# Layer 0's projections as quads of quarter products with a spill to DRAM, and the heads as a second stage

## The chip, the cores and the metric

One Trainium2 chip, of which the kernel uses one core. Times are microseconds of the device for one execution. The engines of a core are named as in the profile: PE is TensorE (matmuls), PEld its weight loads, DVE is VectorE, ACT ScalarE, POOL GpSimd and SP SyncE, whose queue issues most transfers. A mask, a weight or a state lives in SBUF, results of matmuls in PSUM, and everything else in DRAM (HBM).

## The reference

A backbone of two layers over 512 latent tokens (x, 1024 features) and 256 context tokens (ctx). Layer 0 is a retention with four heads, of 256 features for q and k and 512 for v; latent tokens read context and latent tokens in both directions, so that its recurrent form is the same as one product with a mask of decays. Layer 1 is a chunked gMLP with gates. Only x leaves the kernel, so the context passes through layer 0's k and v alone.

```python
for i in range(DEPTH):
    ...
    shift_x, scale_x, gate_x = jnp.split(silu_c @ ada_w[i] + ada_b[i], 3, axis=-1)
    hx = rmsnorm(x, norm_g[i]) * (1 + scale_x[:, None]) + shift_x[:, None]
    hc = rmsnorm(ctx, norm_g[i]) * (1 + scale_c) + shift_c
    ...
    x = x + gate_x[:, None] * out_x
return rmsnorm(x, final_g)

def retention_mixer(hx, hc, w_in, decay_logit, w_out, need_ctx):
    ...
    qc, kc, vc, zc = retention_project(hc, w_in)
    qx, kx, vx, zx = retention_project(hx, w_in)
    qx, kx = axial_rope(qx, row, col), axial_rope(kx, row, col)
    ...
    ox, _, _ = retention_bidirectional(qx, kx, vx, log_g, s_f, s_b)
    out_x = retention_output(ox, zx, w_out)

def retention_output(o, z, w_out):
    o = o * lax.rsqrt(jnp.mean(o * o, axis=-1, keepdims=True) + NORM_EPS)
    ...
    return (o * jax.nn.silu(z)) @ w_out
```

## The kernel before

All data are float32. A factor of a product is split into a high part (a cast to fp32r, on ACT) and a low part (the rest, a subtraction on DVE; `split`, line 86), and `mm3` (line 80) makes each product of three matmuls: low by high, high by low, high by high. So a split of a tile of 128 × 1024 weights costs one operation of ACT and one of DVE.

Weights come in one stream (`Stream`, line 103): a tile is loaded into one of four raw buffers, split into one of four "hl" buffers, two tiles ahead of their use. Layer 0 goes head by head (the loop at line 643). For a head, `proj_v` (414) multiplies the weights of v with the features of x and ctx (`hx`, `hc`, split once), eight steps of 128 over the 1024 features, 512 columns at a time; `proj_z` (433) does the gate's z. `attend` (461) makes scores of 128 keys by 256 queries (twelve for a head, 6 matmuls of 256 columns each), multiplies each with the mask (`pf`), splits it (`phl`), and three scores later multiplies it with v (512 columns); `finish` normalises and gates (`gt`), and `flip` transposes into `og`. `proj_q` of the next head comes next, then `project_out` (535), 96 matmuls of 512 columns for a head (in the last head two halves of 256), whose results DVE adds to the residual `acc`, then `proj_k`. The masks of a head (`decay`, 451) are made by ACT and POOL one head ahead.

The first q and k are made apart, in `proj_qk_first` (339), while layer 0's modulation is still computed: for each of eight blocks of 128 features, PE makes the block's shift and scale (`ada0_mm`, 16 records of `ada_w`), transposes them, and multiplies the finished block with four weight tiles.

In the background (`background`, 590) 32 more tiles of adaLN weights (512 KB each) are loaded one by one and accumulated by DVE (`ada_piece`, 560): a multiplication of 128 × 1024 each, four pieces of eight tiles. They give layer 0's gate and layer 1's shift, scale and gate. `step` moves this on by one tile; it is called once for each weight tile of v and z, and once or twice between.

Layer 1's input projections already use a scheme of seven products in place of eight (`Quads`, 782, and the tables `USES` and `SINGLE`, 776 to 780): both factors are cut into quarters, sums and differences of quarters are formed (T1 to T4 of the weights, S1 to S4 of x), seven products of quarters are made, and their results are combined. The differences of weights, the combinations and the splits fall to DVE and ACT.

The order of the work on PE, ACT and DVE in layer 0 is set by the tile scheduler, which keeps the order of the text only where an engine is marked `kept`; a queue of DMA issues, and each engine, then works its rows in that order.

## Time and profile before

| what | value |
|---|---|
| median of three runs (lowest, highest) | 939.91 us (939.73, 944.60) |
| the profiled execution's own time | 943.52 us |
| its span, first to last instruction | 941.7 us |
| mean granted TensorE clock | 0.989 |
| PE, DVE, ACT, POOL busy | 922.0, 618.5, 385.4, 83.6 us |
| HBM traffic | 117.05 MB read, 8.39 MB written |
| matmuls of PE from 121 to 146 us (the first attention) | 25.00 of 25.00 us busy |

The profile is that of one execution. A row of a group reads: source line, engine, operation, output <- inputs, shapes, how many | busy time, mean ns of one | idle time of the engine just before them, and what ended most of it. Nearly every row has line 53, the helper that records each operation, so groups are told apart by the names of tiles. In a timeline a row gives start and length of a run of like instructions; records of matmuls overlap, so that the rate is read from start to start. In a window a row gives, for each engine, the busy time and the number of instructions, then the granted clock, the DMA share and GB/s.

### The profile page before, as it was taken

To read this page: it belongs to the slowest core of one execution; us is meant where nothing else is said; L and a number is where in the kernel's file an instruction comes from. 1 tells how busy PE (TensorE), PEld (TensorE's weight loads), DVE (VectorE), ACT (ScalarE), POOL (GpSimd) and SP (SyncE) were. 2 spreads that over 40 slices of the span, in tenths; PEclk is the share of its full clock that TensorE was granted. 3 is DMA by queue.
4 is the path that set the end of the run, shared out by engine and by line. 5 is a ranking of instruction groups with operands and counts; after the bars stand their busy time and mean duration, and the time that the engine had idled before them with its cause. 6 is when DMAs were issued, how large, how long until landed. Compare 5 with 4: busy or idle time off the path is not lost.

```text
span 941.7 us, 13689 instructions
## 1 busy us (share of the span) xinstructions
PE 922.0 (98%) x5474; PEld 797.2 (85%) x5474; DVE 618.5 (66%) x895; ACT 385.4 (41%) x606; POOL 83.6 (9%) x64
## 2 busy tenths in 40 slices
PE   8899999999999999999999999899999999999997
PEld 6578887888787887888887899899999899899885
DVE  4575746653348554248454467999999668788975
ACT  4344435222235212344112447755455355244244
POOL 1413102300003100005000000110100000000000
PEclk8899999999999999999999999999999999999999
DMA  9914813544204544205544202474543335136102
GB/s 355 362 63 122 283 74 112 182 133 155 90 1 143 175 141 144 68 1 179 179 134 155 69 23 95 165 256 138 187 136 124 112 99 183 33 113 222 47 23 90
DMA packets 49424, 126.33 MB, mean 134 GB/s; under 512 B 5456, under 2 KB 13776, under 8 KB 49232
## 3 DMA queue, kind: packets, MB, share of 16 engines
q1 hardware_dynamic: 47440, 119.16, 37.8%
q0 software_dynamic: 1920, 6.29, 1.7%
q8 instruction: 43, 0.70, 0.3%
q14 instruction: 21, 0.17, 0.1%
HBM read 117.05 MB, written 8.39 MB: 133 GB/s over the span
## 4 chain that ended last, share of the span: by engine, by line
PE 74%; DMA 10%; DVE 10%; issue 2%; ACT 2%; POOL 1%; SPq 0%; DVEq 0%; POOLq 0%; ACTq 0%
PE pst L53 74%; DMA raw<-in_adag_dram 8%; DVE hl L53 3%; DMA raw<-in_w_dram 1%; DVE rope_t L53 1%; DMA acc<-in_xT_dram 1%; POOL raw L53 1%; ACT hl L53 1%; DVE fz L53 1%; DMA raw<-in_dec_dram 0%; DVE q L53 0%; DVE ada_a L53 0%; ACT f L53 0%; POOL dec L53 0%; DVE ya L53 0%
## 5 line engine op out<-in xcount | busy, mean ns | idle before, releaser
L53 DVE TENSOR_TENSOR hl<-raw,hl 128x1024 fp32r<-128x1024 f32 (+1 forms) x115 | 144.9, 1264 | 66.8 <-ACT hl L53 66.1
L53 ACT CAST hl<-raw 128x1024 fp32r<-128x1024 f32 x115 | 120.1, 1049 | 166.1 <-PE pst L53 94.8
L53 PE MATMUL pst<-hl,hx 128*128 128x512 f32 x696 | 167.4, 395 | 0.9 <-DVE v L53 0.8
L53 PEld LDWEIGHTS pst<-hl,hx 128*128 128x128 f32 x696 | 130.0, 187 | 33.5 <-DVE v L53 2.1
L53 PE MATMUL pst<-hx,hl 128*128 128x512 f32 x384 | 105.1, 407 | 2.0 <-ACT hx L53 1.7
L53 PE MATMUL pst<-hs,hl 128*128 128x256 f32 x768 | 94.7, 282 | 0.0
L53 PEld LDWEIGHTS pst<-hs,hl 128*128 128x128 f32 x768 | 92.4, 188 | 0.3
L53 PE MATMUL pst<-og,hl 128*128 128x512 f32 (+1 forms) x480 | 91.9, 351 | 0.0
L53 PEld LDWEIGHTS pst<-og,hl 128*128 128x128 f32 x480 | 77.0, 188 | 13.8 <-DVE og L53 0.7
L53 DVE SCALAR_TENSOR_TENSOR ada_a<-raw,cpad,ada_a 128x1024 f32<-128x1024 f32 x28 | 37.0, 1320 | 76.9 <-DMA raw<-in_adag_dram 76.8
L53 PEld LDWEIGHTS pst<-hx,hl 128*128 128x128 f32 x384 | 69.0, 192 | 19.6 <-issue 4.4
L53 PE MATMUL pst<-hl,ya 128*128 128x512 f32 x288 | 71.8, 402 | 2.2 <-DVE ya L53 2.2
L53 PE MATMUL pst<-s,hl 128*128 128x256 f32 x576 | 70.5, 280 | 0.0
L53 PEld LDWEIGHTS pst<-s,hl 128*128 128x128 f32 x576 | 69.0, 188 | 0.1
L53 PEld LDWEIGHTS pst<-hl,ya 128*128 128x128 f32 x288 | 55.0, 192 | 15.5 <-DVE ya L53 2.6
L53 POOL TENSOR_TENSOR raw<-raw 128x1024 f32<-128x1024 f32 x12 | 31.8, 2647 | 327.2 <-DMA raw<-in_dec_dram 291.6
L53 PE MATMUL pst<-v,phl 128*128 128x512 f32 x192 | 49.2, 394 | 0.0
L53 DVE SCALAR_TENSOR_TENSOR pf<-pst,dec 128x256 f32<-128x256 f32 x48 | 19.9, 422 | 42.3 <-PE pst L53 42.3
L53 ACT CAST hl<-rx 128x1024 fp32r<-128x1024 f32 x27 | 28.3, 1049 | 29.9 <-DVE rx L53 16.8
L53 PE MATMUL pst<-hl,hs 128*128 128x256 f32 x336 | 40.1, 280 | 0.1
L53 PE MATMUL pst<-hl,hc 128*128 128x512 f32 x156 | 40.1, 395 | 0.0
L53 PEld LDWEIGHTS pst<-hl,hs 128*128 128x128 f32 x336 | 39.5, 188 | 0.3 <-DVE hl L53 0.3
(204 smaller groups left out, 1288.3 us busy)
## 6 DMA issues: line engine op xcount, KB each, us to landing
raw<-in_w_dram SPq DMA_DIRECT2D x64, 512.0 KB, 3.6
raw<-in_w_dram SPq DMA_DIRECT2D x72, 256.0 KB, 3.3
raw<-in_adag_dram SPq DMA_DIRECT2D x32, 512.0 KB, 4.5
raw<-in_dec_dram SPq DMA_DIRECT2D x24, 512.0 KB, 3.6
rx<-in_w_dram SPq DMA_DIRECT2D x36, 256.0 KB, 3.8
ada_w<-in_ada_dram SPq DMA_DIRECT2D x16, 512.0 KB, 8.0
vt<-snap POOLq DMA_DIRECT2D x16, 256.0 KB, 3.8
rkc<-in_w_dram SPq DMA_DIRECT2D x16, 256.0 KB, 3.9
```

The source lines that it names most:

```text
L53: made = op(*args, **kw)
```

## The change

Layer 0's projections become a stage of their own. A list of twelve quads (`QUADS`) goes through the scheme of seven products: one quad for q and k of a head (`features`), two for the halves of v and z of a head (`tokens`). Every product is 24 matmuls of 256 columns. Two of the seven (B11, B21) have a second product beside them with the context as the other factor (`beside`), for k and v of the context. Results are split once (`staged`, four buffers g0 to g3) and stored to DRAM by transfers that POOL issues; for q and k the rotation is done first (`kq_finish`).

The start is rewritten: x is loaded as four quarters, the sums of squares are 48 matmuls of one column (`norm`, three times 16) instead of six, 20 more filling matmuls stand between them, and the loop over the eight blocks of features feeds B11 and B21 of the first three quads, for x (`xs`) and the context (`cs`).

Then the heads follow as a second stage. `load_qk` and `load_v` fetch a head's operands from DRAM, v into the tiles oA11, oS1 and oS2, z into oA12, the same for each head. `attend` makes two scores at a time, 512 columns wide in PSUM (two banks, "tm"), with two such pairs of lag; `project_out` is always two halves of 256 columns, on six banks ("ps"). The adaLN pieces 1 to 3 (24 tiles) move into `attend` and `project_out`, through the two raw buffers w2 and w3; each output weight passes through the raw buffer w0. Masks are made by ACT and DVE; POOL keeps no tensor operation. Layer 1 stays as it was, but for the names of buffers and the common weight stream.

```diff
-            q = proj_q(rest)
-            step(1)
-            dt = st([P, TW], "dec")
-            parts = decay(h + 1, dt)
-            for _ in project_out(og, 1, parts):
-                pass
-            kk_ = proj_k()
...
+    QUADS = (("vz", 0, 0), ("vz", 0, 1), ("vz", 1, 0), ("vz", 1, 1), ("kq", 0), ("vz", 2, 0), ("kq", 1), ("vz", 2, 1),
+             ("kq", 2), ("vz", 3, 0), ("kq", 3), ("vz", 3, 1))
+    first3 = QUADS[:3]
...
+    def tokens(bank, a, w, fresh, ks=range(4)):
+        for kt in ks:
+            r = (w[:, 0, kt * HS:kt * HS + HS], w[:, 1, kt * HS:kt * HS + HS])
+            for t in range(2):
+                l = (a[:, 0, kt, t * P:t * P + P], a[:, 1, kt, t * P:t * P + P])
...
+        def beside(self, name, w):
+            if self.side is None:
+                return
+            if name == "B11":
+                self.c = pt()
+                self.product(self.c, self.side[:, :, 0:4, :], w, True)
+            else:
+                self.product(self.c, self.side[:, :, 4:8, :], w, False)
+                self.done("c", self.c)
...
+    def norm(pair, tags):
+        sqs = [st([P, 4, HS], tag, name="sq0") for tag in tags]
+        act.activation(sqs[0], pair[0], AF.Square)
...
+            for k in range(4):
+                for t in range(2):
+                    mm(p[:, t:t + 1], sqs[g][:, k, t * P:t * P + P], ones[:, 0:1], start=(g, k, t) == (0, 0, 0),
+                       stop=(g, k) == (1, 3), skip_group_check=True)
...
+    def staged(src):
+        t = st([P, 2, 512], f"g{turn[0] % 4}", F32R, name="stg")
+        turn[0] += 1
+        split((t[:, 0, :], t[:, 1, :]), src)
+        return f32(t)
...
+    def kq_finish(h, name, c):
+        if name == "c":
+            spill(kc_d[h], staged(c).rearrange("p a b -> p (a b)"))
+            return
...
+        two = lambda x: x.rearrange("p (m t) -> p m t", m=2)
+        a, b = t2("rope_a"), t2("rope_b")
+        for x, w in ((a, 0), (b, 1)):
+            dve.tensor_tensor(two(x), two(c), rope[:, w, sl].unsqueeze(1).to_broadcast([P, 2, HS]), ALU.mult)
+        dve.tensor_tensor(a[:, 0:HS], a[:, 0:HS], b[:, HS:], ALU.subtract)
+        dve.tensor_tensor(a[:, HS:], a[:, HS:], b[:, 0:HS], ALU.add)
+        spill(dst[h][th], staged(a).rearrange("p a b -> p (a b)"))
...
+    def vz_done(h, fh):
+        fs = slice(fh * HS, fh * HS + HS)
+        def done(name, c):
+            if name in ("11", "21", "c"):
+                dst = vc_d[h] if name == "c" else v_d[h][int(name[0]) - 1]
+                s = staged(c)
+                for x in range(2):
+                    spill(dst[:, x, :, fs], s[:, x, :].rearrange("p (t n) -> p t n", t=2))
+                return
+            act.activation(c, c, AF.Silu)
+            spill(z_d[h][int(name[0]) - 1][:, :, fs], c.rearrange("p (t n) -> p t n", t=2))
...
+    for kb in range(1, 8):
+        if kb == 4:
+            for pr in prods:
+                pr.snap("s1", pr.x)
+        xs(kb)
+        next(n1, None)
...
+    def ada_piece(i, tag, tags):
+        a = st([P, D], tag, name="ada_a")
+        rows = []
+        for k in range(KT + 1):
+            if k < KT:
+                rows.append(bg_raw(tags))
+                load(rows[k], adag_d[8 * i + k])
+            if k == 0:
+                yield None
...
+    def load_qk(h):
+        tags = ("s0", "s1", "s2", "s3", "rope") if h % 2 == 0 else ("w4", "w5", "w6", "g2", "g3")
+        t = [st([P, 2, 2, HS], tag, F32R, name="qk") for tag in tags]
+        for x, src in zip(t, (k_d[h][0], q_d[h][0], k_d[h][1], kc_d[h], q_d[h][1])):
+            load(f32(x).rearrange("p a b c -> p (a b c)"), src)
+        qk[h] = (t[1], t[4]), (t[0], t[2]), t[3]
...
+    def load_v(h):
+        v = [st([P, 2, 2, 512], tag, F32R, name="v") for tag in ("oA11", "oS1", "oS2")]
+        z = st([P, NT, 512], "oA12", name="z")
+        for x, src in zip(v, (*v_d[h], vc_d[h])):
+            load(f32(x), src)
+        for t in range(2):
+            load(z[:, 2 * t:2 * t + 2, :], z_d[h][t])
+        vv[h] = v, z
...
+    for n, q in enumerate(QUADS[3:]):
+        pr = project(q)
+        for i, name in enumerate(SINGLE):
+            pr.run(name, Q.get())
+            if later and i % 2:
...
+            p = pt(tag="tm")
+            for o in range(2):
+                src, jj = key(j + 1 - o)
+                for m in range(2):
+                    l = (src[:, 0, m, jj * P:jj * P + P], src[:, 1, m, jj * P:jj * P + P])
+                    mm3(p[:, o * HS:o * HS + HS], l, (q[hf][:, 0, m, :], q[hf][:, 1, m, :]), m == 0, m == 1)
...
+        LAG = 2
...
+            if i > 2:
+                Q.upto(Q.at + min(i - 1, 5))
+            if i >= LAG:
+                step()
+        return og, flip
...
+    def project_out(og, flip, parts, then=None, between=None, prepare=None):
+        ws = []
+        for hf in range(2):
+            sl = slice(hf * HS, hf * HS + HS)
             for c in range(4):
                 if hf == 0:
...
+                if then is None:
+                    step()
+                    if c == 3:
+                        step()
...
+    for h in range(HEADS - 1):
+        og, flip = attend(h)
+        load_qk(h + 1)
+        load_v(h + 1)
+        project_out(og, flip, decay(h + 1))
+    og, flip = attend(HEADS - 1)
```

By the order of instructions, matmuls of 512 columns go from 2307 to 674, those of 256 from 2689 to 5664, those of one column from 6 to 48 and of 128 from 211 to 237. DVE's operations of 128 × 1024 on two tensors go from 224 to 327, those of 128 × 512 from 213 to 295. POOL loses 36 tensor operations and goes from 24 to 108 DMA issues.

Three places show the new order. First PE in the projections. Before, in and after head 0's attention (v, phl: values; hx, hl: q of head 1; og, hl: the output projection):

```order
L53 MATMUL pst<-q,kc 128x256 x6
L53 MATMUL pst<-v,phl 128x512 x12
L53 MATMUL pst<-vc,phl 128x512 x12
L53 MATMUL pst<-ada_a,ones 32x512 x2
L53 MATMUL pst<-hx,hl 128x512 x24
L53 MATMUL pst<-ident,gt 128x128 x16
L53 MATMUL pst<-hx,hl 128x512 x24
L53 MATMUL pst<-ident,cole 128x64 x4
L53 MATMUL pst<-og,hl 128x512 x96
```

Now, one whole quad of v and z in the first stage (oA and oS are the quarters of x and their sums, hc the context, hl the weights):

```order
L53 MATMUL pst<-oA_190,hl 128x256 x24
L53 MATMUL pst<-hc,hl 128x256 x24
L53 MATMUL pst<-oS_687,hl 128x256 x24
L53 MATMUL pst<-oS_870,hl 128x256 x24
L53 MATMUL pst<-oA_574,hl 128x256 x24
L53 MATMUL pst<-hc,hl 128x256 x24
L53 MATMUL pst<-oS_688,hl 128x256 x24
L53 MATMUL pst<-oS_871,hl 128x256 x24
L53 MATMUL pst<-oA_872,hl 128x256 x24
```

What were runs of 24 to 96 matmuls of 512 columns are now nine products of 24 matmuls of 256, two of them for the context.

Second, DVE where the loop over the blocks of the start has ended. Before, it splits weights and the first kc, and rotates the first q and k:

```order
L53 TENSOR_TENSOR hl_z<-raw,hl_z 128x1024
L53 TENSOR_TENSOR hl_v<-raw,hl_v 128x1024
L53 TENSOR_TENSOR kc<-pst,kc 128x256 x2
L53 TENSOR_TENSOR rope_t<-pst,rope 128x512 x4
L53 TENSOR_TENSOR rope_t<-rope_t 128x512
L53 TENSOR_TENSOR q<-rope_t,q 128x512
L53 TENSOR_TENSOR rope_t<-rope_t 128x512
L53 TENSOR_TENSOR q<-rope_t,q 128x512
L53 TENSOR_TENSOR rope_t<-pst,rope 128x512 x4
L53 TENSOR_TENSOR rope_t<-rope_t 128x512
L53 TENSOR_TENSOR k<-rope_t,k 128x512
L53 TENSOR_TENSOR rope_t<-rope_t 128x512
```

Now (xq are the quarters of x, oS and oA the low parts of their sums, c and stg the first results, combined and split for the store, hl weights):

```order
L53 TENSOR_TENSOR xq<-xq 128x512
L53 TENSOR_TENSOR c_884<-pst,snap 128x512
L53 TENSOR_TENSOR xq<-xq 128x1024
L53 TENSOR_TENSOR oS_687<-xq,oS_687 128x512
L53 TENSOR_TENSOR stg<-c_884,stg 128x512
L53 TENSOR_TENSOR oS_870<-xq,oS_870 128x1024
L53 TENSOR_TENSOR hl<-raw,hl 128x1024
L53 TENSOR_TENSOR stg<-pst,stg 128x512
L53 TENSOR_TENSOR xq<-xq 128x1024
L53 TENSOR_TENSOR oA_872<-xq,oA_872 128x1024
L53 TENSOR_TENSOR c_901<-pst,snap 128x512
L53 TENSOR_TENSOR oS_871<-xq,oS_871 128x1024
```

and directly on, up to the split of the weights of T3 of the first quad:

```order
L53 TENSOR_TENSOR stg<-c_901,stg 128x512
L53 TENSOR_TENSOR stg<-pst,stg 128x512
L53 TENSOR_TENSOR c_913<-pst,snap 128x512
L53 TENSOR_TENSOR stg<-pst,stg 128x512
L53 TENSOR_TENSOR hl<-raw,hl 128x1024
```

The forming of the quarters' sums and the first results of three quads stand ahead of that weight split.

Third, the heads. Before, DVE in the output projection of head 0 (acc: residual; ada_a on raw: adaLN tile; hl: weights):

```order
L53 SCALAR_TENSOR_TENSOR acc<-pst,gate_118,acc 128x512 x2
L53 TENSOR_TENSOR hl<-raw,hl 128x1024
L53 SCALAR_TENSOR_TENSOR acc<-pst,gate_118,acc 128x512 x2
L53 TENSOR_TENSOR hl<-raw,hl 128x1024
L53 SCALAR_TENSOR_TENSOR acc<-pst,gate_118,acc 128x512 x2
L53 TENSOR_SCALAR ada_a<-raw,cpad 128x1024
L53 TENSOR_TENSOR hl<-raw,hl 128x1024
L53 SCALAR_TENSOR_TENSOR acc<-pst,gate_118,acc 128x512 x2
L53 SCALAR_TENSOR_TENSOR ada_a<-raw,cpad,ada_a 128x1024
L53 TENSOR_TENSOR hl<-raw,hl 128x1024
L53 SCALAR_TENSOR_TENSOR ada_a<-raw,cpad,ada_a 128x1024
L53 TENSOR_TENSOR rope_t<-pst,rope 128x512
```

Now, DVE in head 0's attention (pf: score by mask; pl: its low part; ada_a on bg: adaLN tile):

```order
L53 SCALAR_TENSOR_TENSOR pf<-pst,dt 128x512
L53 TENSOR_TENSOR hl<-raw,hl 128x1024
L53 TENSOR_TENSOR pl<-pf,ph 128x512
L53 SCALAR_TENSOR_TENSOR pf<-pst,dt 128x512
L53 SCALAR_TENSOR_TENSOR ada_a<-bg,cpad,ada_a 128x1024
L53 TENSOR_TENSOR pl<-pf,ph 128x512
L53 SCALAR_TENSOR_TENSOR pf<-pst,dt 128x512
L53 SCALAR_TENSOR_TENSOR ada_a<-bg,cpad,ada_a 128x1024
L53 TENSOR_TENSOR pl<-pf,ph 128x512
```

and DVE in the output projection of head 0:

```order
L53 SCALAR_TENSOR_TENSOR acc<-pst,gate_925,acc 128x256 x3
L53 TENSOR_TENSOR og<-pst,og 128x512 x2
L53 SCALAR_TENSOR_TENSOR acc<-pst,gate_925,acc 128x256 x2
L53 SCALAR_TENSOR_TENSOR ada_a<-bg,cpad,ada_a 128x1024
L53 TENSOR_TENSOR dt<-bg 128x512
L53 SCALAR_TENSOR_TENSOR ada_a<-bg,cpad,ada_a 128x1024
L53 TENSOR_SCALAR ada_a<-bg,cpad 128x1024
L53 SCALAR_TENSOR_TENSOR ada_a<-bg,cpad,ada_a 128x1024
L53 SCALAR_TENSOR_TENSOR acc<-pst,gate_925,acc 128x256 x2
L53 COPY sh_927<-pst 128x8
L53 TENSOR_TENSOR sh_927<-sh_927,sv 128x8
L53 TENSOR_TENSOR shs<-sh_927 128x4
```

and the loads on SP's queue for the change from head 0 to head 1 (v, z: head 1's; raw: output weights; bg: adaLN tile or mask):

```order
L108 DMA v<-v_172 128x2048
L108 DMA raw<-in_w_dram 128x1024
L108 DMA v<-v_173 128x2048
L108 DMA v<-vc_179 128x2048
L108 DMA z<-z_184 128x1024
L108 DMA z<-z_185 128x1024
L108 DMA bg<-in_adag_dram 128x1024
L108 DMA bg<-in_dec_dram 128x1024
L108 DMA bg<-in_adag_dram 128x1024 x2
```

The adaLN multiplies, which stood one between two weight splits, now stand up to four together between the residual's additions, and between a score and its low part; their loads stand behind those of the next head's v and z.

1163 lines of the change are left out of this document (555 added, 608 removed).

## The prediction

> **What bounds the kernel now.** I read the table of engines and the slices first, then the chain of waits, then the groups of instructions, and last the timeline and the windows of the stages that the change touches.
>
> ```profile
> PE 922.0 (98%) x5474; PEld 797.2 (85%) x5474; DVE 618.5 (66%) x895; ACT 385.4 (41%) x606; POOL 83.6 (9%) x64
> GB/s 355 362 63 122 283 74 112 182 133 155 90 1 143 175 141 144 68 1 179 179 134 155 69 23 95 165 256 138 187 136 124 112 99 183 33 113 222 47 23 90
> PE 74%; DMA 10%; DVE 10%; issue 2%; ACT 2%; POOL 1%; SPq 0%; DVEq 0%; POOLq 0%; ACTq 0%
> L53 PE MATMUL pst<-hl,hx 128*128 128x512 f32 x696 | 167.4, 395 | 0.9 <-DVE v L53 0.8
> L53 PE MATMUL pst<-hs,hl 128*128 128x256 f32 x768 | 94.7, 282 | 0.0
> ```
>
> TensorE (PE) is busy for 922.0 us of a span of 941.7 waits before almost no group, and carries 74% of the chain that ended last, so work taken from it comes off the time, unless another engine then falls behind. VectorE (DVE) stands at 66%; transfers reached 355 and 362 GB/s in two slices, against a mean of 134.
>
> Since records of matmuls overlap, the price of one comes from stretches without a gap:
>
> ```profile
> 506.53 22.65 PE L53 MATMUL pst<-hl,hx 128*128 128x512 f32 x96
> 529.02 3.03 PE L53 MATMUL pst<-q,k 128*128 128x256 f32 x24
> 555.21 8.68 PE L53 MATMUL pst<-og,hl 128*128 128x256 f32 x72
> 563.72 1.04 PE L53 MATMUL pst<-ident,acc 128*128 128x128 f32 x8
> ```
>
> From start to start, 96 of 512 columns take 22.49 us (0.234 each) and 72 of 256 take 8.51 (0.118 each): half the width costs half the time. A product of quarters, 24 matmuls of 256 columns, is 2.84 us.
>
> How far DVE can be loaded before PE waits is read from the windows:
>
> ```profile
> core 0: us, PE busy (x) PEld busy (x) DVE busy (x) ACT busy (x) POOL busy (x), PEclk, DMA share, GB/s
> 0.00:57.00 57.00, 49.55 (x307) 33.99 (x307) 29.53 (x70) 23.87 (x44) 14.17 (x15) 0.88 0.77 297
> 620.00:740.00 120.00, 119.87 (x998) 118.36 (x998) 114.06 (x162) 60.78 (x81) 7.05 (x13) 1.00 0.50 169
> 756.20:799.40 43.20, 43.20 (x369) 43.20 (x368) 35.87 (x45) 21.48 (x30) 0.00 (x0) 1.00 0.45 146
> ```
>
> Layer 1 already works in products of quarters, and PE stays full with DVE at 83% (756 to 799) and even at 95% (620 to 740).
>
> **PE's work, −30 us.** By the order of instructions the change takes away 1633 matmuls of 512 columns and adds 2975 of 256. By the timeline that is 1633 × 0.234 = 382.6 less and 2975 × 0.118 = 351.6 more, so −31.0; by the groups (167.4/696 = 0.2405, 94.7/768 = 0.1233) −392.7 + 366.8 = −25.9. I take −30, near the stretches without a gap, with −26 and −31 as ends. The Trainium skill (TensorE: Matmul & The Clock Gate, "Wait — 56ns, not 53.3ns?") puts a warm matmul at columns ÷ 2.4 GHz plus about 2.5 ns, a fixed part that narrower matmuls pay more often. An estimate from it, 1633 × 215.8 ns less 2975 × 109.2 ns, is −27.5; the stretches above are slower than the page for both widths, and the saving stays between my ends.
>
> **The start, +8 us (4 to 12).** Its rows:
>
> ```profile
> 12.07 1.66 PE L53 MATMUL pst<-ones,sq 128*128 128x1 f32 x8 [1.72 <-DVE sq L53]
> 26.09 4.75 PE L53 MATMUL pst<-hx,hl 128*128 128x512 f32 x12 [1.72 <-ACT hx L53]
> 39.02 0.96 PE L53 MATMUL pst<-hx,hl 128*128 128x512 f32 x3
> 42.23 1.07 PE L53 MATMUL pst<-ada_w,cpad 128*32 128x256 f32 x16
> 43.24 0.96 PE L53 MATMUL pst<-hx,hl 128*128 128x512 f32 x3
> 44.04 0.38 PE L53 MATMUL pst<-ident,adae 128*128 128x128 f32 x2
> 47.81 0.61 PE L53 MATMUL pst<-ones,sq 128*128 128x1 f32 x4 [0.29 <-POOL sq L53]
> 59.81 5.84 PE L53 MATMUL pst<-hc,hl 128*128 128x256 f32 x48
> ```
>
> Before, a block of the modulation takes 4.22 us (39.02 to 43.24), and by 59.81 the 96 matmuls of x are done, 96 × 0.234 = 22.5 us of useful work; 37.3 us went otherwise. After, a block carries 18 + 18 matmuls of 256 columns (36 × 0.118 = 4.25), the modulation's 1.07 and a transpose's 0.38: 5.7 us, and eight are 45.6. The sums of squares become 48 matmuls of one column instead of 6; two records make one of these, so they cost 0.30 us (47.81) to 0.41 (12.07), and the 16 for the second token half, some 5 us, stand inside the loop. With a first block at about 26, as now, the loop ends near 78 to 80, with 288 × 0.118 = 34 us of useful work done: 80 − 34 − 37.3 = 8.7. I take 8: 4 if the small matmuls fall into what PE idles now (57.00 − 49.55 = 7.45 us), 12 at a block of 6.2 us.
>
> **DVE behind the start, +10 us (4 to 13).** DVE's durations:
>
> ```profile
> L53 DVE TENSOR_TENSOR raw<-raw 128x1024 f32<-128x1024 f32 x18 | 21.9, 1216 | 0.1
> L53 DVE TENSOR_TENSOR snap<-pst,snap 128x512 f32<-128x512 f32 x36 | 24.6, 684 | 2.4 <-PE pst L53 2.1
> L53 DVE SCALAR_TENSOR_TENSOR ada_a<-raw,cpad,ada_a 128x1024 f32<-128x1024 f32 x28 | 37.0, 1320 | 76.9 <-DMA raw<-in_adag_dram 76.8
> ```
>
> In DVE's new order, between the last split of the loop and the weight split of the third product behind the loop (T3), stand ten operations of 512 and seven of 1024 elements: 10 × 0.684 + 7 × 1.216 = 15.4 us. PE has the last ctx block (2.1) and two products of 2.84 to do, 7.8 us, so it waits 7.6. The 15 products left of the three first quads last 42.6 us on PE, while DVE's rows up to their last split hold about 53 us of work: 53 − 2.1 − 40 is some 11, of which the 7.6 is part. I take 10; 13 if the next quads, which DVE meets still behind, add a wait, 4 if DVE begins these operations during the last two blocks.
>
> **The other nine quads, 0.** A pair of quads of both kinds asks DVE for 14 weight splits and 8 differences (22 × 1.216), and some 27 operations of 512 elements (18.5 us): 45 us, beside 18 × 2.84 = 51 us of PE. That is 88%, between the two windows above in which PE was full. What hides it is this surplus of 6 us a pair; with DVE 15% dearer it would be gone. POOL loses its tensor operations and only issues stores; it keeps nobody waiting as long as a store lands within the four staging buffers' turn of several products.
>
> **The second stage, +18 us (5 to 28).** Its rows:
>
> ```profile
> DVE ada_a L53 <- DMA raw<-in_adag_dram: 91.5, 24, 5.1
> raw<-in_adag_dram SPq DMA_DIRECT2D x32, 512.0 KB, 4.5
> L53 DVE SCALAR_TENSOR_TENSOR pf<-pst,dec 128x256 f32<-128x256 f32 x48 | 19.9, 422 | 42.3 <-PE pst L53 42.3
> L53 DVE SCALAR_TENSOR_TENSOR acc<-pst,gate,acc 128x256 f32<-128x256 f32 x16 | 7.4, 478 | 2.3 <-PE pst L53 2.3
> 121.49 3.02 PE L53 MATMUL pst<-q,k 128*128 128x256 f32 x24
> 124.35 1.55 PE L53 MATMUL pst<-v,phl 128*128 128x512 f32 x6
> ```
>
> Now DVE waits 24 times for a tile of adaLN weights, 3.8 us a time, and PE never notices: four raw buffers and the work of four heads lie between, and in an attention (121.49) the scores pass to the values without a gap. After, 24 of these 32 tiles fall into about 100 us of attention and output projection, through two buffers, and behind other loads on SP's queue.
>
> From head 0 to 1: v's three tiles (1 MB each) can load only once the last product with the old v is done, z's two (512 KB) only behind gt; the next adaLN tile (512 KB) stands behind them and a weight tile (512 KB): 5 MB, and 5.24 million bytes at 362 GB/s take 14.5 us. Its multiply stands in DVE's order behind the sixth acc operation, which PE feeds after eight transposes (1.04 us above) and 6 × 1.42 = 8.5 us (1.42 is 12 matmuls at 0.118), at 9.5. So DVE waits there, and every acc behind it, then the next head's pf. Eight more multiplies follow; with two buffers one comes every (4.5 + 1.32) ÷ 2 = 2.9 us: 14.5 + 1.3 + 8 × 2.9 = 39 us to the first pf. PE is through its 23.7 us of output projection (1.04 + 16 × 1.42) and two scores (2.8) at 26.5: up to 12 late, of which I take 10, as some tiles are asked for earlier. The six "ps" banks (8.5 us) only move the wait, since the pf comes last. From head 1 to 2 six multiplies end near 14.5 + 2.6 + 4 × 2.9 = 28.7: 3. From 2 to 3 none is left: 1 for the mask. In head 0's attention the tiles stand behind its v, z and the residual (acc, 2 MB, 5.8 us), which load while the last quad runs out, and their multiplies stand between pf and pl: 4 (0 to 8). Together 18; 5 if only part of it reaches PE, 28 if each of the three transitions costs 8 and the attention 4.
>
> By the fit of the Trainium skill (DMA: Bandwidth & Descriptors, "Anatomy of one DMA": 2.0 us and bytes ÷ 436 GB/s) a tile would land in 3.2 us, an estimate; two buffers would then give one each 2.26 us, PE's own step here, and the sum would be some 6 us lower. The trace has 4.5 for this very load, and that is used.
>
> **The sum.** −30 + 8 + 10 + 0 + 18 = +6: a span of 941.7 becomes 947.7, and the profiled execution's 943.52 (1.8 us lie around the span) becomes 949.5. That execution is 0.4% above the median of the runs, 939.91; on the median's scale I forecast 946 us.
>
> **Rivals.** First, **faster, 931 us**: the waits of the second stage stay on DVE, as the 91.5 us do now. For it: that row, and six banks that cover 8.5 us. The second stage then costs 3 and the rest stands: −30 + 8 + 10 + 3 = −9, so 931; with 6 us behind the start instead of 10, 927. It decides at the first pf of head 1: if that comes less than 2.8 us after PE's last output projection, this case holds. Against it: the 91.5 us were spread over four heads' projections with four buffers, and no six of them stood together ahead of a pf.
>
> Second, **much slower, 961 us**: SP's queue is in order, so a z load waiting for gt holds masks, output weights and q, k of later heads too; each of the three transitions then costs the 14.5 us of its 5 MB whole. 3 × 14.5 − 14 = +29 over my transitions' 14, of which the next attention's slack (25 us of PE against about 15 of DVE) gives back half: 946 + 15 = 961. Against it: output weights are asked for during the attention (four "hl" tiles ahead).
>
> **How the numbers follow.** Forecast 0.54 (its own range 936 to 956), faster 0.32 (922 to 937), much slower 0.14 (955 to 970). Within 0.5%, about what this kernel's measurement can tell, is 935.2 to 944.6: a third of the first case's chance (0.17) and little of the second (0.02). So faster 0.30, same 0.19, slower 0.51. A range of 925 to 965 leaves out less than 0.2.
>
> **What would show it.** PE busy near 890 to 900 and waits of PE at three places: a loop of the start ending near 80, a wait of several us for hl at the first T3, and acc and pf operations behind ada_a waits on the adaLN tiles at the change of heads. The forecast is wrong if PE shows no idle time in the second stage (then the first rival), if matmuls of 256 columns cost more than 0.12 in the new quads, or if DVE cannot keep up with the pairs of quads (a wait for hl at every product, some 6 us more a pair).

## The result, and the profile after

The changed kernel takes 984.40 us (median of four runs, 982.79 to 985.27), the kernel before beside it on the same chip 941.16 (four runs, 939.73 to 944.60): a ratio of 1.0452 with a 95% interval of 1.0417 to 1.0486. The forecast, 946 us and slower, had the side right and the size wrong by 38 us, outside its range. The profiled execution of the changed kernel took 982.79 us with a span of 980.7; the spans differ by 39.0.

The page of the changed kernel: busy time by engine, transfers in 40 slices, and the chain that ended last.

```profile
PE 920.6 (94%) x6950; PEld 870.1 (89%) x6950; DVE 738.5 (75%) x1027; ACT 441.9 (45%) x662; POOL 70.2 (7%) x112
...
GB/s 331 281 58 19 261 205 264 202 147 273 118 230 115 253 132 364 330 313 304 305 291 169 238 136 80 87 166 117 213 109 108 194 81 104 118 108 175 105 23 86
...
PE 64%; DVE 16%; DMA 12%; ACT 5%; issue 3%; SPq 0%; POOL 0%; DVEq 0%; ACTq 0%
```

PE is as long busy as before (920.6 against 922.0), though its matmuls of 256 and 512 columns are worth 31 us less at full speed. The 20 filling matmuls are new (7.3 us in PE's rows), those of one column take 11.8 us instead of 2.3, and matmuls at a lower granted clock count as busy for longer. In the chain PE falls from 74 to 64%, and DVE rises from 10 to 16.

The stages are read from the windows (us, then busy time of PE, PEld, DVE, ACT and POOL, granted clock, DMA share, GB/s):

```profile
26.00:60.00 34.00, 29.46 (x252) 25.45 (x252) 9.75 (x27) 10.23 (x24) 0.00 (x0) 0.90 0.66 229
...
97.00:113.00 16.00, 5.63 (x49) 5.43 (x47) 12.67 (x16) 6.83 (x10) 7.81 (x11) 0.76 0.82 263
113.00:122.00 9.00, 8.57 (x52) 8.60 (x53) 7.14 (x8) 2.96 (x3) 0.00 (x0) 0.68 0.87 276
...
640.00:980.00 340.00, 330.69 (x2424) 312.04 (x2422) 287.73 (x391) 157.64 (x222) 8.11 (x15) 1.00 0.37 123
```

From 113 to 122 us PE is busy for 8.57 of 9.00 us, and still loses time: its mean clock is 0.68. In windows of 1 us the clock is 0.50 up to 118 us and 1.00 from 119 on. Layer 1 (last row) is as it was: from the first product of its weights (624.58) to the end 356.1 us, before 357.5 (584.22 to 941.7).

PE's rows of the start (start, length; in brackets the idle time ahead and what ended it), from the first block to the first product behind the loop:

```profile
33.35 3.92 PE L53 MATMUL pst<-hl,oA 128*128 128x256 f32 x18 [1.11 <-DVE oA L53]
...
40.60 2.40 PE L53 MATMUL pst<-hl,hc 128*128 128x256 f32 x18 [1.89 <-DVE hc L53]
...
45.76 2.40 PE L53 MATMUL pst<-hl,oA 128*128 128x256 f32 x18 [1.54 <-DVE oA L53]
...
53.69 3.63 PE L53 MATMUL pst<-ones,sq 128*128 128x1 f32 x32
...
57.67 1.94 PE L53 MATMUL pst<-ada_w,cpad 128*32 128x256 f32 x16
...
67.56 1.92 PE L53 MATMUL pst<-ada_w,cpad 128*32 128x256 f32 x16 [2.27 <-issue]
...
81.59 2.42 PE L53 MATMUL pst<-hl,oA 128*128 128x256 f32 x18 [1.55 <-DVE oA L53]
...
96.87 5.76 PE L53 MATMUL pst<-hl,oS 128*128 128x256 f32 x48
```

The loop ends at 96.87 and not near 80: by the prediction's own sum 96.87 − 34 − 37.3 = 25.6 us instead of 8. The first block comes at 33.35 instead of 26, and the eight blocks take 63.5 us instead of some 53. The waits in brackets behind the first block make, with the shorter ones between (0.88, 0.41, 0.16), 8.7 us. That of 2.27, which the profile puts down to nothing (issue), is taken up again in the tenth run. Eighteen matmuls that last 2.40 take 3.92 in the first block; the 16 records of ada_w, 1.07 elsewhere, take 1.94 and 1.92 behind the one-column matmuls and behind the wait of 2.27.

Behind the loop, the first T3 of each of the three quads, and what stands in front of the first on ACT and DVE (hl of 109.14: the split of this T3's weights; snap: a product's result, combined):

```profile
105.60 0.58 ACT L53 CAST stg<-pst 128x512 fp32r<-128x512 f32 x1 [3.49 <-DMA vc<-stg]
106.73 0.69 DVE L53 TENSOR_TENSOR stg<-c,stg 128x512 fp32r<-128x512 f32 x1 [3.33 <-ACT stg L53]
...
109.14 1.21 DVE L53 TENSOR_TENSOR hl<-raw,hl 128x1024 fp32r<-128x1024 f32 x1
...
112.61 0.68 DVE L53 TENSOR_TENSOR snap<-pst,snap 128x512 f32<-128x512 f32 x1
...
113.43 8.30 PE L53 MATMUL pst<-hl,oS 128*128 128x256 f32 x48 [10.80 <-DVE snap L53]
...
132.22 7.40 PE L53 MATMUL pst<-hl,oS 128*128 128x256 f32 x48 [2.09 <-DVE snap L53]
...
149.09 5.84 PE L53 MATMUL pst<-hl,oS 128*128 128x256 f32 x48 [1.07 <-DVE snap L53]
...
388.89 3.03 PE L53 MATMUL pst<-qk 128*128 128x256 f32 x24
```

PE had ended at 102.63. The weights of T3 were split 7.7 us later, at 110.35. What ended the wait was the `snap` that ends at 113.29: T3 goes into the same PSUM tile as the product before it, and DVE had still to read that product's result.

The fifteen products end three products behind the last T3, at 149.09 + 8.5 = 157.6. That is 60.7 us for 42.6 of work: 18.1 lost, of which 14.0 are waits and 4.0 slow matmuls (8.30 and 7.40 where 5.84 is usual). The nine later quads run from 157.6 to the first scores at 388.89, 231.3 us for 81 × 2.84 = 230.

The second stage, 388.89 to 624.58: PE's waits by what ended them (total, times, longest), then the rows of the three large ones, then what stands in front of them on ACT and DVE:

```profile
PE pst L53 <- DVE ada_a L53: 9.4, 1, 9.4
PE pst L53 <- DVE pl L53: 7.7, 3, 6.4
PE pst L53 <- DVE pf L53: 3.0, 3, 2.3
```

```profile
404.65 0.79 PE L53 MATMUL pst<-v,pl 128*128 128x512 f32 x1 [6.45 <-DVE pl L53]
...
443.31 1.92 PE L53 MATMUL pst<-ada_a,ones 128*32 128x512 f32 x4 [9.38 <-DVE ada_a L53]
...
466.00 2.15 PE L53 MATMUL pst<-qk 128*128 128x256 f32 x12 [2.31 <-DVE pf L53]
...
401.69 1.04 ACT L53 CAST hl<-raw 128x1024 fp32r<-128x1024 f32 x1 [8.80 <-DMA raw<-in_w_dram]
402.64 0.61 ACT L53 CAST ph<-pf 128x512 fp32r<-128x512 f32 x1
...
436.98 1.28 DVE L53 SCALAR_TENSOR_TENSOR ada_a<-bg,cpad,ada_a 128x1024 f32<-128x1024 f32 x1 [2.52 <-DMA bg<-in_adag_dram]
...
438.54 1.28 ACT L53 ACT_TABLE_LOAD   x1 [6.76 <-DMA bg<-in_dec_dram]
...
441.20 0.69 DVE L53 TENSOR_TENSOR dt<-bg 128x512 f32<-128x512 f32 x1 [2.94 <-ACT bg L53]
441.97 1.28 DVE L53 SCALAR_TENSOR_TENSOR ada_a<-bg,cpad,ada_a 128x1024 f32<-128x1024 f32 x1
```

Waits make 21 us here (with 1.0 of small ones), matmuls at a low clock behind them about 6. The first, in head 0's attention, is not one for adaLN: ACT waits 8.80 us to cast an **output weight** tile, and the cast of the score (ph) stands behind it in ACT's order. The second is one for adaLN, but not through acc or pf: PE's **own row**, the four matmuls that sum a finished adaLN piece over the partitions (`columns`), stands in the middle of the output projection and waits for the last multiply of its piece (441.97), with more than half of head 0's output projection behind it. That multiply is itself late by the **mask** of head 1: the operation ahead of it on DVE (dt, 441.20) waits for ACT, and ACT had waited 6.76 us for the mask's tile (438.54). From the end of the multiply before (438.26) to 441.97, 3.7 of the 9.38 us pass so.

Why the weight tile was late shows in the transfers of 360 to 405 us (40 slices of 1.1 us; then KB and median time from issue to landing):

```profile
GB/s 404 62 0 0 15 0 58 277 422 335 313 102 375 433 408 313 269 269 361 426 426 408 415 411 415 430 419 419 411 419 426 419 419 412 419 404 415 422 244 51
...
acc<-in_xT_dram SPq DMA_DIRECT2D x4, 512.0 KB, 14.0
...
bg<-in_adag_dram SPq DMA_DIRECT2D x3, 512.0 KB, 12.6
...
raw<-in_w_dram SPq DMA_DIRECT2D x2, 512.0 KB, 10.2
```

For 20 us and more the transfers run flat at some 420 GB/s: head 0's v and z, the next q, the residual, adaLN and weights all at once. A tile of 512 KB, whose median over the whole execution is 4.4 to 4.6 us, takes 10 to 14 here, and the late weight tile itself 16.6 (asked for at 385.04, cast at 401.69):

```profile
bg<-in_adag_dram SPq DMA_DIRECT2D x32, 512.0 KB, 4.6
...
raw<-in_w_dram SPq DMA_DIRECT2D x16, 512.0 KB, 4.4
```

The Trainium skill (HBM Reference, "Specifications (TRN2)") gives about 425 GB/s for a core that streams alone; the flat part agrees with it.

In sum: −31 (PE's work) + 25.6 + 18.1 + 1 + 27 − 1.4 (layer 1) = +39, the measured difference of the spans.

### The profile page after: what moved, and what is told of

Its sections match the earlier page's. It is cut to its first block, busy times and chain, and to the rows that moved or that the text cites. A ratio compares the mean times of both kernels' runs of the same rounds, so it can differ in the third digit from the quotient of the medians.

```text
span 980.7 us, 17185 instructions
## 1 busy us (share of the span) xinstructions
PE 920.6 (94%) x6950; PEld 870.1 (89%) x6950; DVE 738.5 (75%) x1027; ACT 441.9 (45%) x662; POOL 70.2 (7%) x112
## 4 chain that ended last, share of the span: by engine, by line
PE 64%; DVE 16%; DMA 12%; ACT 5%; issue 3%; SPq 0%; POOL 0%; DVEq 0%; ACTq 0%
PE pst L53 64%; DMA raw<-in_w_dram 5%; DVE hl L53 4%; DMA bg<-in_adag_dram 3%; DVE raw L53 2%; ACT hl L53 1%; DMA bg<-in_dec_dram 1%; DVE ada_a L53 1%; DVE ya L53 1%; DVE snap L53 1%; DMA vt<-vt 1%; DVE f L53 1%; DMA ada_w<-in_ada_dram 1%; DMA vc<-stg 1%; DVE oS L53 1%
## 5 line engine op out<-in xcount | busy, mean ns | idle before, releaser
L53 DVE TENSOR_TENSOR hl<-raw,hl 128x1024 fp32r<-128x1024 f32 x198 | 239.4, 1220 | 77.2 <-ACT hl L53 76.4
L53 PE MATMUL pst<-hl,oS 128*128 128x256 f32 x1152 | 141.8, 284 | 14.0 <-DVE snap L53 14.0
L53 PEld LDWEIGHTS pst<-hl,oS 128*128 128x128 f32 x1152 | 139.8, 193 | 15.3 <-issue 11.0
L53 PE MATMUL pst<-oS,hl 128*128 128x256 f32 x1152 | 140.6, 281 | 1.3 <-DVE hl L53 1.3
L53 PEld LDWEIGHTS pst<-oS,hl 128*128 128x128 f32 x1152 | 138.1, 188 | 1.6 <-ACT ya L53 1.6
L53 DVE TENSOR_TENSOR raw<-raw 128x1024 f32<-128x1024 f32 x96 | 116.3, 1219 | 3.6 <-DMA raw<-in_w_dram 2.6
L53 PE MATMUL pst<-hl,oA 128*128 128x256 f32 x816 | 104.4, 285 | 5.9 <-DVE oA L53 4.6
L53 PE MATMUL pst<-oA,hl 128*128 128x256 f32 x864 | 108.6, 282 | 0.0
L53 PEld LDWEIGHTS pst<-hl,oA 128*128 128x128 f32 x816 | 100.3, 192 | 7.8 <-DVE oA L53 5.6
L53 PEld LDWEIGHTS pst<-oA,hl 128*128 128x128 f32 x864 | 105.1, 189 | 0.3
```

The costliest lines, as they stand in the source:

```text
L53: made = op(*args, **kw)
```

## Experiments

Each is the changed kernel with one edit, unless it says otherwise. Four numbers place a saving: the end of the loop, the first scores, the first product of layer 1, and the span; the changed kernel has 96.87, 388.89, 624.58 and 980.7. Those without an interval are single executions.

The first number scatters. In six executions whose start has the same rows of PE in the same order (the changed kernel and the third, fourth, fifth, sixth and eleventh runs below) the loop ends between 92.69 and 100.35 us. Their waits in the loop are 8.7 us each time. The granted clock differs: from 12 to 33 us it is 0.67 in the changed kernel and 0.84 in the third run, whose first block comes at 29.34. So a difference of less than some 4 us at this number, taken from one execution each, shows nothing.

**The start: filling matmuls.** The filling ahead of the first block seemed to delay it by 7 us.

```diff
-    fill(4)
-    fill(16)
```

> Edit: the 20 filling matmuls between the sums of squares (4 and 16) are left out; nothing else. Theory A (PE's own row order sets the start: the 16 fillers, 5.2 us at half clock, and the context's 16 squares, 3.6 us, stand ahead of the first block of products, which begins at 33.35): the first block begins near 28, the loop ends near 91 instead of 96.9, and the execution is 5 to 6 us shorter. Rival (ACT's order sets it: the first block's cast stands behind the context's root, and the fillers only pass the time): the first block still begins after 32 and the time stays within 2 us, or grows because the granted clock is lower.

Measured: 984.62 us; 94.36, 387.03, 624.56, 982.6. The first block begins at 26.77, but the blocks behind it are slower (PE's rows of this run):

```profile
26.77 4.21 PE L53 MATMUL pst<-hl,oA 128*128 128x256 f32 x18 [2.88 <-DVE oA L53]
...
34.83 3.74 PE L53 MATMUL pst<-hl,hc 128*128 128x256 f32 x18 [1.90 <-DVE hc L53]
...
55.83 3.96 PE L53 MATMUL pst<-hl,hc 128*128 128x256 f32 x18
```

Of 6.6 us gained at the first block 2.5 are left at the end of the loop, less than the scatter, and none at the end. The waits of the loop are the same 8.7 us, and the clock from 26 to 60 us is 0.76 instead of 0.90. So no gain from an earlier first block is shown: without filling, the time goes into a lower clock.

**The start: sums of squares.** POOL adds the squares of the context and of the second token half, so that two matmuls do for sixteen, twice.

```diff
-        for g in range(2):
-            for k in range(4):
+        s = sqs[0]
+        if few:
+            nc.gpsimd.tensor_tensor(s, s, sqs[1], ALU.add)
+            nc.gpsimd.tensor_tensor(s[:, 0:2, :], s[:, 0:2, :], s[:, 2:4, :], ALU.add)
+            nc.gpsimd.tensor_tensor(s[:, 0:1, :], s[:, 0:1, :], s[:, 1:2, :], ALU.add)
+        for g in range(1 if few else 2):
+            for k in range(1 if few else 4):
```

> Edit: the squares of the context and of the second token half are first summed over the feature blocks on POOL (three additions), so that 2 matmuls of one column take the place of 16, twice. Theory A (the 32 extra one-column matmuls lie on PE's path): 3.63 us becomes about 0.5 twice, -6 us by the end of the loop. Rival (the loop is held by the chain from the modulation's transposes over DVE and ACT to the split, and POOL's sums of some 5 us come late for the root): 0, or some us slower.

Measured: 976.76; 89.80, 380.04, 617.67, 975.0. The loop ends 7.1 us earlier, of which 5.7 reach the end. With the scatter the gain is nearer 5: the four executions with these sums and the old filling (second, eighth, ninth and tenth runs) end the loop at 89.68 to 94.14, 91.8 in the mean, the six without them at 96.6. So these small matmuls are about a fifth of the start's 25.6.

**Second stage: adaLN.** Pieces 1 and 2 are multiplied in the first stage, beside the quads, and piece 3 from head 2 on.

```diff
-            for a in ada_piece(i, *(("s0", ("s1", "s2")) if i == 0 else ("oA22", ("w2", "w3")))):
+            for a in ada_piece(i, *(("s0", ("s1", "s2")) if i < 3 else ("oA22", ("w2", "w3")))):
...
-            if q[0] == "vz" and i % 2 and not piece0:
-                if step() == 0:
+            if not piece0:
+                if step() == 2:
...
-            if i >= LAG:
+            if i >= LAG and h >= 2:
...
-                if then is None:
+                if then is None and h >= 2:
```

> Edit: adaLN pieces 1 and 2 are accumulated in the first stage, one tile after each product of the nine later quads, and piece 3 starts with head 2; same results. Theory A: PE's waits in the change from head 0 to 1 (9.4 us before the row with ones and ada_a, 2.3 before the scores, and the lower clock behind each, about 3 us) go, -14 us; the wait of 6.45 us in head 0's attention stays, since it is a weight tile that is late there. The forecast's mechanism (adaLN multiplies ahead of pf and pl everywhere): that wait goes too, -22. Rival: DVE, 88% full in the quads, cannot carry 16 more multiplies (21 us), PE waits there for weight splits, and the gain is given back: 0.

Measured: 963.52; 92.69, 387.41, 603.32, 961.8. The waits of 9.4 and 2.3 are gone, and the second stage takes 215.9 us instead of 235.7. The nine later quads, with 16 more multiplies and PE's sums of two pieces, take 236.4 us instead of 231.3, 1.2 of it waits. So 14.7 of the 19.8 us are a net gain; of the 18.9 us by which the span is shorter, 4.2 lie in the start, which the edit doesn't touch. The wait in head 0's attention stays, with 6.02 for 6.45, though only two multiplies are left there, both done by 390.2, and no load of adaLN: adaLN does not make it.

**Head 0's attention: the residual's load.** Its 2 MB are asked for four steps later in the text.

```diff
-            if (h, i) == (0, 2):
+            if (h, i) == (0, 6):
```

> Edit: the load of the residual (2 MB) is asked for four steps later in head 0's attention, so that the first output weight tile is no longer behind all of it on SP's queue. Theory A (that weight tile is late, ACT's cast of it stands ahead of the cast of the second pair of scores, and pl waits): the wait of 6.45 us falls under 1, -7 to -9 us with the clock behind it. Rival (the forecast: adaLN multiplies between pf and pl): the wait stays near 6 and the time within 2 us.

Measured: 976.87; 95.18, 387.14, 618.82, 975.0. The second stage is 4 us shorter; the wait moves one pair of scores ahead and is still ACT's wait for the weight tile (ACT's and PE's rows of this run):

```profile
393.04 1.04 ACT L53 CAST hl<-raw 128x1024 fp32r<-128x1024 f32 x1 [7.14 <-DMA raw<-in_w_dram]
...
395.94 2.93 PE L53 MATMUL pst<-qk 128*128 128x256 f32 x12 [5.78 <-DVE pf L53]
```

By SP's queue the edit does less than was meant: in the changed kernel the tile is asked for (385.04) behind all four loads of the residual, here (382.28) behind one of them, with two others directly after it. The traffic is no less, 417 GB/s from 380 to 402 us against 415. The tile still lands 8.6 us earlier (6.9 against the first scores), 10.7 us after it was asked for instead of 16.6. So what stood ahead of it made a part of its delay; the forecast that the wait falls under 1 us missed, and a tile that lands in time was not tried. What PE waits for is the cast in ACT's order.

**PE's own row.** The sums of adaLN pieces 1 and 2 are put off by four steps; the loads and multiplies stay.

```diff
-    def columns(a, dst):
+    def columns(a, dst, wait=0):
+        for _ in range(wait):
+            yield
...
-                yield from columns(a, sh1)
+                yield from columns(a, sh1, 4)
-                yield from columns(a, gs1)
+                yield from columns(a, gs1, 4)
```

> Edit: after the last multiply of adaLN pieces 1 and 2 the background waits four more steps before PE's rows that sum the piece over the partitions. Theory A (those rows stand in PE's own order between two output projections and wait for the piece, 9.4 us at 443): PE runs on into the six banks, that wait falls under 2 us, and the execution is 5 to 8 us shorter, since pf of head 1 is then late by some us more. The forecast's mechanism alone (acc and pf are late, PE's own row is not the point): the wait moves behind the sixth bank or to the first pf of head 1 and the time stays within 2 us.

Measured: 979.87 (before, on that chip: 942.34); 100.35, 392.94, 618.07, 977.8. The second stage takes 225.1, 10.6 us less, with the adaLN tiles as late as ever. The start came 3.5 us later in this execution, which its edit doesn't touch. PE's sum now runs without a wait, at 449.30. So the 9.4 us hang on the place of four matmuls in PE's order.

**Behind the start.** The first results of quads 2 and 3 are combined, split and stored behind the first two T3.

```diff
-    for i, pr in enumerate(prods):
+    def drained(pr):
...
+    drained(prods[0])
...
+                if name == "T3" and i < 2:
+                    drained(prods[i + 1])
```

> Edit: the first results of the second and third quad (c11 and the context's) are combined, split and stored while the quad before them runs, not all ahead of the first T3. Theory A (ten operations and a wait for a staging buffer stand ahead of T3): the wait of 10.8 us at the first T3 falls to 3 to 6, but the work comes later, so that the waits at the next T3 rows grow; end of the three quads 4 to 6 us earlier. Rival (DVE's whole work bounds these 60 us, 56 of them busy): the wait only moves, and the time stays within 2 us.

Measured: 978.34; 96.95, 381.67, 618.61, 976.3. From the loop's end to the scores 7.3 us are saved; the wait at the first T3 falls from 10.80 to 3.80, those at the next two are 1.56 and 1.81. The matmuls behind the shorter wait are as slow as before (PE's row of this run):

```profile
106.51 8.39 PE L53 MATMUL pst<-hl,oS 128*128 128x256 f32 x48 [3.80 <-DVE snap L53]
```

**Is DVE too full there?** POOL makes the weight differences of the first three quads instead of DVE.

```diff
-                    dve.tensor_tensor(r, raw(uses[0]), raw(uses[1]), ALU.subtract)
+                    (nc.gpsimd if q in first3 else dve).tensor_tensor(r, raw(uses[0]), raw(uses[1]), ALU.subtract)
```

> Edit: POOL makes the differences of weights (T1 to T4) of the first three quads, 12 operations of 128 x 1024 that DVE made. If DVE's whole work bounds the stretch behind the start: it has 14.6 us less, and the three quads end 8 to 14 us earlier. Rival (the staging buffers and the order hold it): the wait at the first T3 stays near 10 and the gain is under 4; POOL's 2.65 us for each may also be late.

Measured: 995.18; 97.92, 400.82, 635.90, 993.4. Worse by 12.7: the wait at the first T3 is 11.34, and another of 8.67 appears. Taking 12 operations of 1.2 us from DVE removes no wait. But the run does not separate DVE's load from POOL's lateness: POOL takes 2.6 us for each, waits for weight tiles, and its stores stand behind (POOL's row of this run):

```profile
117.56 5.16 POOL L166 TENSOR_TENSOR raw<-raw 128x1024 f32<-128x1024 f32 x2 [4.00 <-DMA raw<-in_w_dram]
```

**The edits together.** First the squares on POOL, adaLN early, results late, and POOL's differences.

> Edit: e2, e3, e6 and e7 together. If their parts are separate: -6 -19 and 8 to 14 behind the start, so 940 to 948 us; if the gain behind the start is given back by DVE in the quads, which then also carry the adaLN multiplies: 952 to 958.

Measured: 973.81; 89.68, 398.02, 615.19, 972.0. POOL's differences take back what the others bring: 3.79, 10.52, 4.50 and 2.51 us of waits behind the start.

Then without them, and with the output weights of heads 0 and 1 loaded through three raw buffers in place of one:

```diff
-            Q.load((("wo", h, c), "w"), W[:1], 1, [(whole, w_d[16 * h + 12 + c])])
+            Q.load((("wo", h, c), "w"), W[:1] + (W[2:4] if h < 2 else []), 1, [(whole, w_d[16 * h + 12 + c])])
```

> Edit: e2, e3 and e6 together, and the output weights of heads 0 and 1 may also use the raw buffers w2 and w3, so that the first of them is loaded ahead of the residual. Theory A (start, stretch behind it, adaLN rows and the late weight tile are separate costs): -6 -19 -5 to -7 and, for the wait of 6.45 us in head 0's attention and the clock behind it, -8: a span of 940 to 944, the same as the kernel before within 0.5%. If the weight tile is still late because the transfers at the change of stage run at their limit (over 400 GB/s), that wait stays and the span is near 950. Rival (gains given back by DVE in the quads): over 955.

Measured, three rounds: 953.68, ratio to the kernel before 1.0112 (1.0066 to 1.0157); 93.65, 382.25, 593.85, 955.2. The second stage takes 211.6 us, and head 0's wait falls from 6.45 to 2.60: with three buffers the tiles are asked for earlier, and the cast that waits for a late one (ACT stands 7.57 us) comes one pair of scores later. Three quarters of the loss are gone.

The wait of 2.27 us in the start (a PSUM bank that DVE still reads as the broadcast of the norm) was then taken up by a copy on ACT:

```diff
+        if few:
+            src, pr = pr, t2("rsb", (P, HS))
+            act.copy(pr, src)
```

> Edit: e9, and for the context and the second token half the broadcast of the norm is copied from PSUM to SBUF by ACT before DVE multiplies with it, so that the PSUM bank comes free after 0.4 us and not after DVE's 2.35. Theory A (PE's wait of 2.27 us before the modulation's rows in the loop is for that bank): -2 to -4 against e9. Rival (ACT's queue is as late as DVE's): within 1 us of e9, or slower.

Measured, three rounds: 956.98, ratio 1.0147 (1.0092 to 1.0202); 94.14, 383.81, 595.64, 953.9. The 2.27 become 0.24, and three rows later PE waits 2.70 us for an ACT operation. No gain.

**The clock.** Forty filling matmuls on PE inside the wait at the first T3, on the changed kernel:

```diff
+                if i == 0 and name == "T3":
+                    again(40)
```

> The changed kernel with 40 filling matmuls of 128 columns (about 10 us) on PE ahead of the first T3, where PE otherwise waits 10.80 us. Theory A, the clock falls because PE pauses: the two T3 products behind them take about 5.8 us instead of 8.30, the granted clock between 113 and 122 us is above 0.9 instead of 0.70, and the first q and k product comes 2 to 4 us earlier (385 to 387 instead of 388.89). Rival, the clock falls for another reason (the transfers of that time, or work per us as such): the T3 products still take over 7.5 us and the milestone stays within 1 us, or is later by what the filling runs over.

Measured: 985.47; 97.82, 393.89, 627.06, 983.6. PE's rows around the filling:

```profile
103.42 9.09 PE L53 MATMUL pst<-ones 128*128 128x128 f32 x80
...
114.43 5.84 PE L53 MATMUL pst<-hl,oS 128*128 128x256 f32 x48 [1.92 <-DVE snap L53]
...
123.63 5.49 PE L53 MATMUL pst<-hl,oA 128*128 128x256 f32 x24 [3.36 <-DVE snap L53]
```

The window of the T3 products in the same kernel:

```profile
113.00:122.00 9.00, 5.84 (x48) 5.67 (x48) 5.60 (x7) 1.85 (x2) 0.00 (x0) 1.00 0.83 244
```

The clock is 1.00 from 113 to 122 us where it was 0.68, and the two T3 products take 5.84 us instead of 8.30, beside much the same transfers (244 GB/s against 276): the pause lowers the clock, and filling prevents it. But nothing is gained: from the loop's end to the first scores it is 296.1 us instead of 292.0. PE is through its T3 products 1.5 us earlier, though the loop ended 0.95 us later, and then waits 3.36 us for DVE, which waits for a weight tile (3.40 us; 1.59 in the changed kernel); behind this pause the next product is slow. So the first theory is right on the clock and the rival on the time: the slow matmuls lay under DVE's lateness.

At last the four edits with the filling spread over the waits: none ahead of the first block, six matmuls ahead of each of the blocks 1 to 4, twelve ahead of the first T3.

```diff
-    fill(4)
-    fill(16)
...
+        if kb < 5:
+            again(6)
         xs(kb)
...
+                if i == 0 and name == "T3":
+                    again(12)
```

> The four edits together again (squares of the context and the second token half summed on POOL, adaLN pieces 1 and 2 in the first stage, results of quads 2 and 3 combined later, output weights of heads 0 and 1 through three raw buffers), but the 20 early filling matmuls are taken out and others stand where PE waits: six ahead of each of the blocks 1 to 4 of the start, twelve ahead of the first T3. Theory A, filling belongs into the waits: the first block starts near 27 us as without early filling, and the clock no longer falls behind it, so the loop ends near 88 instead of 93.65 and the time is about 948, near the kernel before. Rival, the blocks of the start are bound by the chain of modulation, split and PSUM bank, not by PE's clock: the loop ends at 92 to 95 whatever is filled, and the time stays at 952 to 957.

Measured, three rounds: 952.39, ratio 1.0103 (1.0047 to 1.016); 89.19, 378.84, 591.27, 947.8 (the profiled execution is the shortest of the four, 949.61). PE's rows at the first two blocks and the loop's end, for this kernel:

```profile
27.28 4.17 PE L53 MATMUL pst<-hl,oA 128*128 128x256 f32 x18 [1.10 <-DVE oA L53]
...
39.94 2.41 PE L53 MATMUL pst<-hl,oA 128*128 128x256 f32 x18
...
89.19 5.76 PE L53 MATMUL pst<-hl,oS 128*128 128x256 f32 x48
```

The first block comes as early as without filling, and the clock of the loop's first half rises from 0.84, with the four edits alone, to 0.92:

```profile
26.00:60.00 34.00, 27.50 (x220) 23.29 (x220) 13.38 (x28) 10.48 (x24) 4.47 (x3) 0.84 0.65 229
```

```profile
26.00:60.00 34.00, 28.66 (x251) 25.08 (x255) 14.60 (x32) 12.13 (x27) 4.39 (x3) 0.92 0.64 230
```

The loop ends 4.5 us earlier than in the ninth run, near what the first theory gave. That the filling did it is not shown: with the old filling and the same sums on POOL it ended at 89.80 and 89.68 in the second and eighth runs. In the medians the difference is 1.3 us, and the intervals of the two overlap.

No version beats the kernel before; the best two stand 1.0 and 1.1% above it. In the last one the start still costs 89.19 − 34 − 37.3 = 17.9 us, and 7.4 of it are waits of the loop, most of them for DVE's and ACT's chain of modulation and split. Whether this chain can be made shorter was not tried.

## Why the prediction was right or wrong

**PE's work, −30: right.** Products of quarters take 2.84 us in the new quads, 0.118 a matmul.

**The start, +8 (4 to 12): the largest error; it is 25.6.** The block of 5.7 us was right where nothing waits (83.85 to 89.56). Two steps failed. "With a first block at about 26, as now" took over the old start although the prediction had itself counted 48 small matmuls for 6 and had no term for the 20 filling matmuls (7.3 us). Nor is 26 where the old products began: the first of x stand at 21.44, and 26.09 is a later row. The block came at 33.35, and even at 26.77 (no filling) no gain is shown. And the eight blocks were priced as if PE worked through them at full clock: the loop held 8.7 us of waits and lost some 4.5 to a lower clock; only its one-column matmuls (3.6 us) were in the sum, at some 5. The small matmuls were to fall into the 7.45 us that PE idled up to 57 us, at the low end of the range; up to 57 us PE now idles 8.6 us. By runs, the squares are shown as some 5 us. The clock's part and the waits are read from the trace; only one wait was moved, and no run shows what filling saves. The 25.6 us are those of one execution: with the scatter of the loop's end they are 21 to 29.

**DVE behind the start, +10 (4 to 13): the place right, the size 18.1.** The wait at the first T3 was given as 7.6, up to the split of its weights, and is 10.80. That split came 7.7 us behind PE's last product, nearly as forecast, but by luck: DVE began its rows before the loop ended, and the 15.4 us were summed without their waits. ACT stands 3.49 us for a staging buffer whose store has not landed, and DVE 3.33 behind ACT. The other 3.1 us are a step that the prediction left out: the result of the product before T3 has to be read first (`snap`), and stands behind the next weight split on DVE. The prediction had dismissed the wait for a store ("it keeps nobody waiting as long as a store lands within the four staging buffers' turn"): that turn is several products long in the later quads, but here six results come at once for four buffers. Late results (sixth run: 3.80 instead of 10.80) show the order as the cause of some 7 us of this wait. The other 4.0 us are slow matmuls behind the waits, for which the sum had no term.

**The other nine quads, 0: right** (231.3 for 230). With 16 more multiplies of adaLN and PE's sums beside them (third run) they wait 1.2 us.

**The second stage, +18 (5 to 28): 27, the cause only half right.** That adaLN among the heads costs PE time is shown: with pieces 1 and 2 moved to the quads the second stage is 19.8 us shorter, 14.7 net. But the path was another. The prediction let the multiplies delay acc and pf; the 9.4 us came by PE's own sums of a piece, four matmuls for which it had no term, as the fifth run shows. About 3.7 of them were the mask's tile and ACT's work on it, ahead of the last multiply on DVE; the prediction priced a mask at 1 us, and only from head 2 to 3. This share is read from the trace, and no run tested it. The 2.31 us at the next scores (pf) are the part that came by the path of the prediction. Head 0's attention lost 6.45 us, not 4, and not by adaLN: an output weight, cast by ACT ahead of the scores, landed late among transfers of some 420 GB/s (third, fourth and ninth runs). From 480 us on 2.1 us of waits are left in this stage, where 4 were forecast for the later changes of heads. The rival of 931, that the waits stay on DVE, fell with these rows. That of 961, with 14.5 us at each of three transitions, has its size at one transition only, and by another path. The measured 984 lies above every case that was given a chance.

**Missing altogether:** what a wait costs behind it. After each wait of more than 2 us in these places of the changed kernel's profile PE's next matmuls ran at half the clock for some 3 to 5 us (0.50 in windows of 1 us from 114 to 118 and from 133 to 135). By rows that is some 14 us in the three places together, though in the eleventh run filling one of the waits brought none of it back.

## What to carry to other kernels

When work is taken from the engine that bounds a kernel, go through each stage row by row for what now ends last there: the engine's own small rows in text order, other engines' in-order rows that wait for a transfer, and buffers that come free only with a store. A saving spread over the whole span can be lost in three places where new work is dense, as here. And price a pause of PE with the slow matmuls behind it, and a late load by what lands in the same 20 us, not by its mean over the execution.

## What the runs showed of the hardware

A run of one-column matmuls, with no idle time at all (53.69, 3.63 us, 32 records), is followed by matmuls at a lower clock (16 records in 1.94 us instead of 1.07), as a pause is. With 4 records in its place (second run, 0.50 us) the same 16 take 1.07.

The Trainium skill (TensorE: Matmul & The Clock Gate, "What's actually happening") has the clock fall to half after an idle window of about 3.4 us and rise after a busy one as long; the trace agrees in kind, but not in length. At the longest wait the clock, in windows of 1 us, falls to 0.50 some 2.6 us after PE's last matmul and is 1.00 again some 5.4 us after its next one. That waits of 2.09 and 2.31 us cost speed as well (7.40 for 5.84, 2.15 for 1.58) is more than that rule says. Nor is the price fixed by the wait's length: the wait of 1.89 us ahead of the first block of the context is followed by 18 matmuls in 2.40 us in the changed kernel and in 3.92 in the fifth run, and that of 2.27 by 16 records in 1.92 and, in the twelfth run, in 1.07.

Transfers held 404 to 430 GB/s for 20 us, with loads and stores mixed. The 362 GB/s by which the prediction priced a change of heads is a mean over a slice of 23.5 us: in finer slices the kernel before held 404 to 439 GB/s too, for 19 us of its start. While the transfers ran so, a tile of 512 KB, which lands in 4.4 us in the median, took 10 to 16.6 us.
